# Hybrid encoder trunk: a fourth group of seven products in each FFN in place of blocks 4 and 5

## The chip, the cores and the metric

The kernel runs on one core of one Trainium2 chip. The metric is device microseconds (us) of one execution; three executions of the kernel before were timed, and a fourth was recorded by the profiler.

## The reference, cut to what matters

A trunk of two layers over 256 tokens of width 1024, all in float32. Each layer has a mixing part (two attention branches, merged) and a gated FFN with 2816 hidden columns. The change lies in the FFN alone:

```python
gate, up = jnp.split(rms_norm(h, g_ffn_pre) @ w_ffn_in, 2, axis=-1)
h = h + rms_norm((jax.nn.silu(gate) * up) @ w_ffn_out, g_ffn_post)
```

`w_ffn_in` is 1024 x 5632 (gate and up beside each other), `w_ffn_out` is 2816 x 1024. The hidden columns are cut into 11 blocks of 256, numbered 0 to 10.

## The kernel before, in words

**Three matmuls for one.** To keep float32 accuracy each operand is held as a high and a low part. The high part is a cast by ACT (`split`, line 113, in the trace `CAST wh_..`), the low part a subtraction by DVE (line 109, `TENSOR_TENSOR wl_..`). A product of two such operands is three matmuls: high by high, high by low, low by high (`mm3`). Every weight that comes from memory passes through ACT and then DVE in this way, in two halves of 1024 columns each.

**Units.** Weights come in units of 1 MB, 128 partitions by 2048 columns. A stream (`Stream`, named `ws`) loads them in the order of a list, `plan`. A plain load goes into one of two buffers (`raw_..`), so that a load waits until the unit two places ahead has been split. The split parts lie in four buffers each (`wh_..`, `wl_..`); a unit's buffers come free when PE has used it. `ws.depth` and `ws.held` keep at most four of them in use.

**The three kinds of work in the FFN.** The letters in the string `FFN` give their order; a `p` only loads a few small tensors.

- `u`: half of a plain block of `w_ffn_in` (one of two units), 24 matmuls of 128x512.
- `o`: one unit of `w_ffn_out` (`out_step`), 24 matmuls, 12 for each half of the tokens. It reads a block of the hidden activations, transposed, which `hid.need` fetches; which block is the next is set by `OUT`.
- `1` to `7`: a group of seven products (`seven`), which does two blocks (a pair, named by its first) in the manner of Strassen and Winograd: 7 products of 12 matmuls in place of 8. The activations' four combined forms are made once (`sums`). The weights' combinations are made in place, in `Stream.step`: with the four units of a pair called x, z (first half of the rows, gate and up), q and y (second half), the unit x is split for product 1, z is added to it by DVE (line 292), it is split again for product 2, y is added by DVE, it is split for product 3, then q is added to it from memory by an accumulating DMA of GpSimd (line 308, two halves), and it is split a last time for product 7. Product 4 uses y, product 6 uses q, product 5 uses z, to which y has been added by another accumulating DMA (line 295).

x and z have no buffers of their own: they are lent one of the four `wh` and one of the four `wl` buffers (in the trace `lent_..`). The `lend` flag lets the next pair's x and z be loaded only behind the split for product 7 of the pair before. y has a buffer of the kind `big_..`, and q one of the two `raw_..` buffers.

A pair's result is gated on ACT and DVE (lines 1339 and 106), turned by a DMA transpose (line 414) with copies by ACT before and behind it (lines 408 and 427), and split (`big_0ffnin`) for the `o` that reads it. `tick` and `need` decide where this is written in the program; the last pair (`PAIRS[-1]`) is turned by PE instead.

In each layer the blocks 0 and 1 come first, outside of the string. Before the change, 4, 5 and 10 are plain, and the groups start at 2, 6 and 8. What of `OUT` has not been used inside the string (three units) follows behind it, as `ffnout`.

**What sets the order.** Dependencies are found by the tile framework, and a scheduler writes each engine's instructions in one fixed order. On the chip each engine runs its own list in that order.

Of the kernel before, what the change touches and what calls it, by code (L numbers as in the profile page):

```python
# [34 lines left out]

FFN = "uu1u2u34u567" "uo12o34o5o67" "poo12o345o67"
MERGE = "GGGG1G2G34G5G67gggg"
PLAIN, PAIRS = (4, 5, 10), (2, 6, 8)  # L40
OUT = (0, 1, 2, 3, 4, 5, 10, 6, 7, 8, 9)

WAIT_LAST = (3, 4)
SENT, LANDED, NEXT = 3, 9, 2
# [7 lines left out]
def trunk_kernel(ctx: ExitStack, tc: tile.TileContext, a: dict, out: bass.AP):  # L52
# [87 lines left out]
    def unit(w, kh, c0):  # L140

        return lambda t: [
            (
                t[:, :2048].rearrange("p (k c) -> p k c", c=512),
                w[kh * 512 : (kh + 1) * 512, c0 : c0 + 512].rearrange("(k p) c -> p k c", p=P),
            )
        ]
# [24 lines left out]
            )  # L172
        ]

    plan = []
    for l in range(DEPTH):
        w = a["w_in"][l]
        plan += [unit_rows(w, n, C_RA, C_RA + 1056, 2 if l + n == 0 else 1) for n in range(4)]
        for c0 in (C_AK, C_GQ, C_GK, C_GV, C_GV + 512, C_GG, C_GG + 512):
            plan += [unit(w, kh, c0) for kh in range(2)]  # L180
        gates = [unit(w, kh, c0) for c0 in (C_GA, C_GA + 512, C_GB, C_GB + 512) for kh in range(2)]
        glas = [unit(a["w_o_gla"][l], kh, j * 512) for j in range(2) for kh in range(2)]
        pair = [unit(a["w_o_attn"][l], kh, j * 512) for kh in range(2) for j in range(2)]
        for x in MERGE:
            plan.append(gates.pop(0) if x == "G" else glas.pop(0) if x == "g" else (pair, int(x)))
        plan += [unit(a["w_out"][l], kh, j * 512) for kh in range(2) for j in range(2)]
        w = a["w_ffn_in"][l]
        blocks = [[unit_gate_up(w, kh, b) for kh in range(2)] for b in range(NBLK)]
        plan += blocks[0] + blocks[1]
        plains = [u for b in PLAIN for u in blocks[b]]  # L190
        pairs = [[unit(w, kh, c + b * 256) for kh in range(2) for c in (0, HIDDEN)] for b in PAIRS]
        outs = [unit_rows(a["w_ffn_out"][l], n) for n in OUT]
        for x in FFN.replace("p", ""):
            if x == "1":
                pair = pairs.pop(0)
            plan.append(plains.pop(0) if x == "u" else outs.pop(0) if x == "o" else (pair, int(x)))
        plan += outs
        plan += [unit_rows(a["w_ple_proj"][l], 0)]
        plan += [unit(a["w_ple_gate"][l], kh, j * 512) for kh in range(2) for j in range(2)]
# [14 lines left out]
    class Stream:  # L214
# [8 lines left out]
        def __init__(self, depth):  # L223
            self.depth, self.held, self.room, self.ready, self.open = depth, 0, 0, [], False
            self.loads, self.jobs, self.lend = [], [], False
            pairs = {}
            for item in plan:
                if callable(item):
                    x = Load(item)
                    self.loads.append(x)  # L230
                    self.jobs.append(lambda x=x: self.plain(x))
                else:
                    units, n = item
                    if n == 1:
                        b11, b12, b21, b22 = units
                        x, z = (Load(b, lambda tag=tag: self.lent(tag), tag == "wh") for b, tag in ((b11, "wh"), (b12, "wl")))
                        y, q = Load(b22, big), Load(b21)
                        pairs[id(units)] = x, y, z, q
                        self.loads += [x, y, z]
                    if n == 5:  # L240
                        self.loads.append(q)
                    self.jobs.append(lambda p=pairs[id(units)], n=n: self.step(n, *p))

        def lent(self, tag):

# [40 lines left out]
            for piece in self.put(x):  # L286
                self.cast = split(*piece)

        def step(self, n, x, y, z, q):
            def add(to, other):  # L290
                c = slice(0, 2048)
                nc.vector.tensor_tensor(out=to.raw[:, c], in0=to.raw[:, c], in1=other.raw[:, c], op=ALU.add)

            def sent(to, src):
                nc.gpsimd.dma_start(to.raw[:, :2048], src, accum_op=ALU.add)

            if n == 7:
                self.load()
            self.made((x, x, x, y, z, q, x)[n - 1])
            if n == 1:  # L300
                add(x, z)
                sent(z, y.raw[:, :2048])
            elif n == 2:
                add(x, y)
            elif n == 3:
                for dst, src in q.make(x.raw):
                    for c in (slice(0, 2), slice(2, 4)):
                        nc.gpsimd.dma_start(dst[:, c], src[:, c], accum_op=ALU.add)
            elif n == 7:
                self.held -= 1  # L310
                self.lend = True
# [499 lines left out]
    for l in range(DEPTH):  # L811
# [561 lines left out]
        steps, pairs, seven_ = chain.from_iterable(block(b) for b in PLAIN), list(PAIRS), None  # L1373
        for x in FFN:
            if x == "p":
# [6 lines left out]
            if x == "o":  # L1382
                n, w = outs.pop(0), ws.take()
# [118 lines left out]
```

## Time and profile before

| what | us |
|---|---|
| median of three executions (lowest, highest) | 918.69 (918.22, 921.97) |
| the profiled execution: its own time | 921.25 |
| the profiled execution: span from the first to the last instruction | 919.1 |
| PE busy in the span | 904.6 |
| DVE busy | 737.2 |
| ACT busy | 643.9 |
| GpSimd busy | 112.4 |

The page gives for each engine how long it was busy in the span. A busy PE is counted from the start of the first to the modelled end of the last of matmuls that overlap, so two neighbouring matmuls must be compared by their starts. Rows of the timeline have the start, the duration, the engine, the line, the operation, what is written and read, and, in brackets, how long the engine had been idle and what ended it. Layer 0's FFN runs from about 256 to 433 us, and its part with the groups from 280 to 415 us.

### The profile page before, as it was taken

Reading aid. Unit: us, or ns where it says so; the run is one execution under the profiler, and the core shown is the slowest. Engines: PE = TensorE matmul, PEld = TensorE weight load, DVE = VectorE, ACT = ScalarE, POOL = GpSimd, SP = SyncE. Lnnn points to the kernel's source line nnn. Section 1 sums busy time; section 2 is a strip of 40 time slices with the busy share of each in tenths; the row PEclk is TensorE's granted clock in tenths of the full one; section 3 lists DMA queues with packets and bytes.
Section 4 is the critical chain, followed back from the end, with each engine's and each line's share of the span. In section 5 each row is a group of like instructions: output and inputs, shape, how many; then the busy total and the mean of one; then the engine's idle time right before and its main releaser. Section 6 shows DMA issues by size and latency. Waiting matters only on the chain.

```text
span 919.1 us, 12313 instructions
## 1 busy us (share of the span) xinstructions
PE 904.6 (98%) x4561; PEld 768.3 (84%) x4561; DVE 737.2 (80%) x947; ACT 643.9 (70%) x1032; POOL 112.4 (12%) x174
## 2 busy tenths in 40 slices
PE   8999999999999999999999999999999999999996
PEld 6999888888888888888899988888888788878786
DVE  4798987977679796888689789688786798968874
ACT  4658777964568796776665686878656787957663
POOL 2410201140010100010023002111001010101000
PEclk9999999999999999999999999999999999999999
DMA  6555356986489998966555524399675999979541
GB/s 218 182 193 180 117 163 231 229 241 234 144 243 256 279 273 250 301 194 240 184 176 184 190 91 148 128 290 234 208 247 173 274 230 290 261 284 243 200 167 46
DMA packets 123290, 193.38 MB, mean 210 GB/s; under 512 B 33431, under 2 KB 56471, under 8 KB 122206
## 3 DMA queue, kind: packets, MB, share of 16 engines
q1 hardware_dynamic: 117726, 175.81, 59.3%
q0 software_dynamic: 5504, 16.78, 10.1%
q8 instruction: 36, 0.59, 0.3%
q14 instruction: 24, 0.20, 0.1%
HBM read 175.80 MB, written 1.05 MB: 192 GB/s over the span
## 4 chain that ended last, share of the span: by engine, by line
PE 80%; ACT 6%; DMA 5%; DVE 4%; issue 2%; POOL 2%; SPq 0%; POOLq 0%; ACTq 0%; DVEq 0%
PE acc_0ffnin L97 10%; PE acc_1ffnin L97 10%; PE acc_0ffnin L581 5%; PE acc_1gate L97 5%; PE acc_0gate L97 5%; PE acc_1ffnin L581 4%; PE acc_1gqk L97 3%; PE acc_0rq L97 2%; PE acc_0gqk L97 2%; PE acc_1ple L97 2%; PE acc_1gg L97 2%; PE acc_0gg L97 2%; PE acc_0v L97 2%; PE acc_1v L97 2%; PE acc_1merge L97 2%; PE acc_0merge L97 2%
## 5 line engine op out<-in xcount | busy, mean ns | idle before, releaser
L97 PE MATMUL acc_1ffnin<-wh_1ffnin,big_1ffnin 128*128 128x512 f32 x176 | 56.5, 392 | 0.1
L97 PE MATMUL acc_0ffnin<-wh_0ffnin,big_0ffnin 128*128 128x512 f32 x176 | 56.2, 391 | 0.0
L109 DVE TENSOR_TENSOR wl_1ffnin<-raw_1ffnin,wh_1ffnin 128x1024 fp32r<-128x1024 f32 x38 | 44.9, 1220 | 12.3 <-ACT wh_1ffnin L113 12.3
L109 DVE TENSOR_TENSOR wl_0ffnin<-raw_0ffnin,wh_0ffnin 128x1024 fp32r<-128x1024 f32 x38 | 44.9, 1221 | 10.5 <-ACT wh_0ffnin L113 10.2
L113 ACT CAST wh_1ffnin<-raw_1ffnin 128x1024 fp32r<-128x1024 f32 x38 | 38.3, 1050 | 17.7 <-DMA raw_1ffnin<-in_w_ffn_out_dram 9.1
L113 ACT CAST wh_0ffnin<-raw_0ffnin 128x1024 fp32r<-128x1024 f32 x38 | 38.4, 1050 | 16.8 <-DMA raw_0ffnin<-in_w_ffn_out_dram 7.8
L109 DVE TENSOR_TENSOR wl_1ffnin<-lent_1ffnin,wh_1ffnin 128x1024 fp32r<-128x1024 f32 x30 | 35.5, 1220 | 4.9 <-ACT wh_1ffnin L113 4.7
L109 DVE TENSOR_TENSOR wl_0ffnin<-lent_0ffnin,wh_0ffnin 128x1024 fp32r<-128x1024 f32 x30 | 35.5, 1221 | 4.8 <-ACT wh_0ffnin L113 4.7
L97 PEld LDWEIGHTS acc_1ffnin<-wh_1ffnin,big_1ffnin 128*128 128x128 f32 x176 | 33.0, 188 | 7.2 <-ACT wh_1ffnin L113 0.5
L97 PEld LDWEIGHTS acc_0ffnin<-wh_0ffnin,big_0ffnin 128*128 128x128 f32 x176 | 33.0, 188 | 6.9 <-DVE big_0ffnin L109 0.2
L113 ACT CAST wh_1ffnin<-lent_1ffnin 128x1024 fp32r<-128x1024 f32 x30 | 30.3, 1049 | 8.6 <-issue 2.9
L113 ACT CAST wh_0ffnin<-lent_0ffnin 128x1024 fp32r<-128x1024 f32 x30 | 30.3, 1050 | 8.4 <-issue 2.9
L97 PE MATMUL acc_1ffnin<-wl_1ffnin,big_1ffnin 128*128 128x512 f32 x88 | 34.4, 391 | 0.8 <-DVE wl_1ffnin L109 0.8
L97 PE MATMUL acc_0ffnin<-wl_0ffnin,big_0ffnin 128*128 128x512 f32 x88 | 34.5, 392 | 0.3 <-DVE wl_0ffnin L109 0.3
L581 PE MATMUL acc_0ffnin<-wh_0ffnin,mid_0ffnin 128*128 128x512 f32 x96 | 31.0, 390 | 0.0
L581 PE MATMUL acc_1ffnin<-wh_1ffnin,mid_1ffnin 128*128 128x512 f32 x96 | 31.0, 390 | 0.0
L97 PE MATMUL acc_0ffnin<-wh_0ffnin,big_0wout 128*128 128x512 f32 x96 | 30.4, 389 | 0.0
L97 PE MATMUL acc_1ffnin<-wh_1ffnin,big_1wout 128*128 128x512 f32 x96 | 30.3, 389 | 0.0
L97 PE MATMUL acc_0rq<-wh_start,big_start 128*128 128x384 f32 (+1 forms) x96 | 25.4, 350 | 1.5 <-ACT big_start L124 1.5
L97 PE MATMUL acc_1rq<-wh_0ple,big_0ple 128*128 128x384 f32 (+1 forms) x96 | 23.5, 325 | 0.0
L581 PE MATMUL acc_1ffnin<-wh_1ffnin,big_1wout 128*128 128x512 f32 x72 | 23.1, 389 | 0.0
L581 PE MATMUL acc_0ffnin<-wh_0ffnin,big_0wout 128*128 128x512 f32 x72 | 23.1, 389 | 0.0
(745 smaller groups left out, 3011.7 us busy)
## 6 DMA issues: line engine op xcount, KB each, us to landing
raw_0ffnin<-in_w_ffn_out_dram SPq DMA_DIRECT2D x11, 1024.0 KB, 5.1
raw_1ffnin<-in_w_ffn_out_dram SPq DMA_DIRECT2D x11, 1024.0 KB, 5.1
lent_0ffnin<-in_w_ffn_in_dram SPq DMA_DIRECT2D x6, 1024.0 KB, 7.5
lent_1ffnin<-in_w_ffn_in_dram SPq DMA_DIRECT2D x6, 1024.0 KB, 6.0
raw_0rq<-in_w_in_dram SPq DMA_DIRECT2D x4, 1024.0 KB, 5.1
raw_0v<-in_w_in_dram SPq DMA_DIRECT2D x4, 1024.0 KB, 5.1
raw_0merge<-in_w_out_dram SPq DMA_DIRECT2D x4, 1024.0 KB, 5.2
raw_0wout<-in_w_ffn_in_dram SPq DMA_DIRECT2D x8, 512.0 KB, 4.6
```

The lines of the kernel that those rows point to most:

```text
L97: return nc.tensor.matmul(o, lhsT, rhs, start=start, stop=stop)
L109: nc.vector.tensor_tensor(out=out, in0=in0, in1=in1, op=ALU.subtract)
L113: cast = nc.scalar.copy(hi, src)
L581: nc.tensor.matmul(o, x, y, start=first and k + n == 0, stop=k == 3 and n == 2, skip_group_check=not first)
```

## The change

Two constants of order are new, and a switch for how q is added:

```diff
-FFN = "uu1u2u34u567" "uo12o34o5o67" "poo12o345o67"
+FFN = "uu12o34o567" "o123o4567" "po123o4567" "o123o4567"
-PLAIN, PAIRS = (4, 5, 10), (2, 6, 8)
-OUT = (0, 1, 2, 3, 4, 5, 10, 6, 7, 8, 9)
+PLAIN, PAIRS = (10,), (2, 4, 6, 8)
+ADDED = (2, 4, 6, 8)
+OUT = (0, 1, 10, 2, 3, 4, 5, 6, 7, 8, 9)
...
-            elif n == 3:
+            elif n == 3 and far:
                 for dst, src in q.make(x.raw):
                     for c in (slice(0, 2), slice(2, 4)):
                         nc.gpsimd.dma_start(dst[:, c], src[:, c], accum_op=ALU.add)
+            elif n == 5 and not far:
+                add(x, q)
```

`far` is true for a pair that is in `ADDED`, and for the pair in the merge. All four pairs of the FFN are in `ADDED`, so every pair has its q added by the DMA, as before, and the last branch is never taken.

Blocks 4 and 5 become a fourth pair. In each layer 2 plain blocks (4 units, 96 matmuls) give way to 7 products (84 matmuls). The first group now has two `u` and two `o` between its products, the other three have one `o` ahead of product 1 and one between products 3 and 4. Three units of `w_ffn_out` are left for behind the string, as before.

The lists of the engines show the passage from one group to the next. The first place is DVE in layer 0, from the split for product 7 of the second group to the split for product 4 of the third. Before, `wl_0ffnin_3353` is product 7, `3359` and `3411` are two `o`, `3441`, `3482`, `3542` and `3566` are products 1 to 4, `3513` is an `o`, and lines 292 are the two additions:

```order
L109 TENSOR_TENSOR wl_0ffnin_3353<-lent_0ffnin_3023,wh_0ffnin_3352 128x1024 x2
L109 TENSOR_TENSOR wl_0ffnin_3359<-raw_0ffnin_3305,wh_0ffnin_3358 128x1024 x2
L625 TENSOR_TENSOR mid_0ffnin_3179<-acc_0ffnin_3396,mid_0ffnin_3179 128x512
L109 TENSOR_TENSOR wl_0ffnin_3411<-raw_0ffnin_3350,wh_0ffnin_3410 128x1024 x2
L106 TENSOR_TENSOR t_0ffnin_3418<-mid_0ffnin_3180,t_0ffnin_3418 128x512
L109 TENSOR_TENSOR wl_0ffnin_3441<-lent_0ffnin_3364,wh_0ffnin_3440 128x1024 x2
L106 TENSOR_TENSOR t_0ffnin_3435<-mid_0ffnin_3179,t_0ffnin_3435 128x512
L292 TENSOR_TENSOR lent_0ffnin_3364<-lent_0ffnin_3364,lent_0ffnin_3368 128x2048
L109 TENSOR_TENSOR wl_0ffnin_3482<-lent_0ffnin_3364,wh_0ffnin_3481 128x1024 x2
L292 TENSOR_TENSOR lent_0ffnin_3364<-lent_0ffnin_3364,big_0ffnin_3366 128x2048
L109 TENSOR_TENSOR wl_0ffnin_3513<-raw_0ffnin_3370,wh_0ffnin_3512 128x1024 x2
```

Now product 7 is `wl_0ffnin_3199`, `3205` the one `o` that follows, `3248`, `3278`, `3318` and `3364` are products 1 to 4, and `3343` is the `o` between 3 and 4 (the lines of the code have moved by one to six):

```order
L110 TENSOR_TENSOR wl_0ffnin_3199<-lent_0ffnin_2975,wh_0ffnin_3198 128x1024 x2
L110 TENSOR_TENSOR wl_0ffnin_3205<-raw_0ffnin_3108,wh_0ffnin_3204 128x1024 x2
L110 TENSOR_TENSOR mid_0ffnin_3085<-mid_0ffnin_3085,acc_0ffnin_3087 128x512
L631 TENSOR_TENSOR mid_0ffnin_3085<-acc_0ffnin_3233,mid_0ffnin_3085 128x512
L107 TENSOR_TENSOR t_0ffnin_3255<-mid_0ffnin_3086,t_0ffnin_3255 128x512
L110 TENSOR_TENSOR wl_0ffnin_3248<-lent_0ffnin_3210,wh_0ffnin_3247 128x1024 x2
L107 TENSOR_TENSOR t_0ffnin_3272<-mid_0ffnin_3085,t_0ffnin_3272 128x512
L296 TENSOR_TENSOR lent_0ffnin_3210<-lent_0ffnin_3210,lent_0ffnin_3214 128x2048
L110 TENSOR_TENSOR wl_0ffnin_3278<-lent_0ffnin_3210,wh_0ffnin_3277 128x1024 x2
L296 TENSOR_TENSOR lent_0ffnin_3210<-lent_0ffnin_3210,big_0ffnin_3212 128x2048
L110 TENSOR_TENSOR wl_0ffnin_3318<-lent_0ffnin_3210,wh_0ffnin_3317 128x1024 x2
L110 TENSOR_TENSOR wl_0ffnin_3343<-raw_0ffnin_3216,wh_0ffnin_3342 128x1024 x2
```

One `o` is gone from between products 7 and 1, and the `o` from between the second addition and product 3. The subtraction that takes product 5's sum out of `acc_0ffnin_3087`, into which PE then adds product 7, now stands behind the split of the `o`.

The second place is ACT at the same passage: the casts for products 2 and 3, and the copies of the sums that PE has finished. Before, `wh_0ffnin_3481` is the cast for product 2, `3512` for an `o`, `3541` for product 3; L629 and L632 copy out products 1 and 2:

```order
L113 CAST wh_0ffnin_3481<-lent_0ffnin_3364 128x1024 x2
L113 CAST wh_0ffnin_3512<-raw_0ffnin_3370 128x1024 x2
L427 COPY mid_0ffnin_3459<-mid_0ffnin_3459 128x2x512
L629 COPY mid_0ffnin_3520<-acc_0ffnin_3522 128x512
L113 CAST big_0ffnin_3537<-mid_0ffnin_3459 128x4x128
L113 CAST wh_0ffnin_3541<-lent_0ffnin_3364 128x1024 x2
L427 COPY mid_0ffnin_3473<-mid_0ffnin_3473 128x2x512
L632 COPY mid_0ffnin_3520<-acc_0ffnin_3523 128x512
```

Now L635 and L638 are these copies, `wh_0ffnin_3277` and `3317` the casts for products 2 and 3, `3342` that for the `o`, `3363` and `3386` those for products 4 and 5, and `big_0ffnin_3382` the second group's result, which this `o` reads:

```order
L635 COPY mid_0ffnin_3325<-acc_0ffnin_3327 128x512
L114 CAST wh_0ffnin_3277<-lent_0ffnin_3210 128x1024 x2
L638 COPY mid_0ffnin_3325<-acc_0ffnin_3328 128x512
L114 CAST wh_0ffnin_3317<-lent_0ffnin_3210 128x1024 x2
L114 CAST wh_0ffnin_3342<-raw_0ffnin_3216 128x1024 x2
L114 CAST wh_0ffnin_3363<-big_0ffnin_3212 128x1024 x2
L433 COPY mid_0ffnin_3295<-mid_0ffnin_3295 128x2x512
L640 COPY mid_0ffnin_3326<-acc_0ffnin_3327 128x512
L114 CAST big_0ffnin_3382<-mid_0ffnin_3295 128x4x128
L114 CAST wh_0ffnin_3386<-lent_0ffnin_3214 128x1024 x2
```

The copies of products 1 and 2 now stand ahead of the casts for products 2 and 3, where before each stood behind the cast of the product that follows it.

The third place is PE, a little further on. Before, PE ran the `o` of the string whole. Now the `o` behind product 3 (`wh_0ffnin_3342`) starts when half of product 4 (`wh_0ffnin_3363`) is done:

```order
L587 MATMUL acc_0ffnin_3328<-wl_0ffnin_3364,mid_0ffnin_2712 128x512
L587 MATMUL acc_0ffnin_3328<-wh_0ffnin_3363,mid_0ffnin_2712 128x512
L98 MATMUL acc_0ffnin_2860<-wh_0ffnin_3342,big_0ffnin_3382 128x512
L98 MATMUL acc_0ffnin_2860<-wl_0ffnin_3343,big_0ffnin_3382 128x512
L98 MATMUL acc_0ffnin_2861<-wh_0ffnin_3342,big_0ffnin_3382 128x512
```

Its first 12 matmuls run there, and its other 12, for the second half of the tokens, behind most of the rest of product 4. In the second to fourth groups PE also runs 12 matmuls of the `o` that follows a group between products 6 and 7. Layer 1 has the same lists but for a place or two.

More of the change, by code (lines that the diff above doesn't have):

```diff
@@ L173, in unit_rows @@
         ]
-    plan = []
+    plan, added = [], []
     for l in range(DEPTH):
@@ L183, in trunk_kernel @@
         pair = [unit(a["w_o_attn"][l], kh, j * 512) for kh in range(2) for j in range(2)]
+        added.append(id(pair))
         for x in MERGE:
@@ L195, in trunk_kernel @@
                 pair = pairs.pop(0)
+                if PAIRS[-1 - len(pairs)] in ADDED:
+                    added.append(id(pair))
             plan.append(plains.pop(0) if x == "u" else outs.pop(0) if x == "o" else (pair, int(x)))
@@ L241, in __init__ @@
                         self.loads.append(q)
-                    self.jobs.append(lambda p=pairs[id(units)], n=n: self.step(n, *p))
+                    self.jobs.append(lambda p=pairs[id(units)], n=n, f=id(units) in added: self.step(n, f, *p))
         def lent(self, tag):
@@ L287, in made, with step @@
                 self.cast = split(*piece)
-        def step(self, n, x, y, z, q):
+        def step(self, n, far, x, y, z, q):
             def add(to, other):
```

## The prediction

> **What bounds the kernel now.** I read the page's first lines, then who PE waits for, then the stretch with the groups by windows, and last the timelines of PE, DVE and ACT around one passage between two groups.
>
> ```profile
> span 919.1 us, 12313 instructions
> PE 904.6 (98%) x4561; PEld 768.3 (84%) x4561; DVE 737.2 (80%) x947; ACT 643.9 (70%) x1032; POOL 112.4 (12%) x174
> ```
>
> PE is busy 98% of the span: PE sets the time. In the windows with the groups (279 to 415 us in layer 0, 740 to 866 in layer 1) PE's waits are these alone:
>
> ```profile
> PE acc_0ffnin L97 <- DVE wl_0ffnin L109: 0.3, 1, 0.3
> PE acc_1ffnin L97 <- DVE wl_1ffnin L109: 0.8, 1, 0.8
> ```
>
> So 0.3 and 0.8 us: splits arrive in time. But not by much, as the windows of layer 0's three groups show (columns: length, then busy time of PE, PEld, DVE, ACT, POOL, granted clock, DMA share, GB/s):
>
> ```profile
> 279.00:326.00 47.00, 47.00 (x209) 38.91 (x209) 41.19 (x45) 38.10 (x53) 3.42 (x3) 1.00 0.97 255
> 326.00:373.00 47.00, 46.73 (x207) 38.38 (x206) 38.18 (x38) 34.68 (x42) 3.29 (x3) 1.00 0.92 282
> 373.00:415.00 42.00, 42.00 (x189) 34.78 (x188) 37.22 (x34) 31.44 (x36) 4.31 (x4) 1.00 0.85 235
> ```
>
> DVE works 37 to 41 of 42 to 47 us, ACT 31 to 38, and the DMA share is 0.85 to 0.97. PE is the bound, with three others close behind. What decides is the passage between groups. PE in the third group, first matmuls of product 6 of the group before, then of products 1, 2 and of the `o` behind them:
>
> ```profile
> 367.78 0.39 PE L581 MATMUL acc_0ffnin<-wh_0ffnin,big_0wout 128*128 128x512 f32 x1
> ...
> 384.10 0.39 PE L581 MATMUL acc_0ffnin<-wh_0ffnin,big_0wout 128*128 128x512 f32 x1
> ...
> 386.82 0.39 PE L581 MATMUL acc_0ffnin<-wh_0ffnin,mid_0ffnin 128*128 128x512 f32 x1
> ...
> 389.54 0.39 PE L97 MATMUL acc_0ffnin<-wh_0ffnin,big_0ffnin 128*128 128x512 f32 x1
> ```
>
> From 384.10 to 386.82 there are 12 matmuls: 2.72 us for a product, 0.227 for a matmul, 5.44 for a unit of 24. Product 7 began at 367.78 + 2.72 = 370.50. DVE for the same passage: the split for product 7, for product 1, a gating, the first addition, the split for product 2, the second addition, a split of transposed results, and the split for product 3:
>
> ```profile
> 366.30 2.35 DVE L109 TENSOR_TENSOR wl_0ffnin<-lent_0ffnin,wh_0ffnin 128x1024 fp32r<-128x1024 f32 x2
> ...
> 375.82 2.36 DVE L109 TENSOR_TENSOR wl_0ffnin<-lent_0ffnin,wh_0ffnin 128x1024 fp32r<-128x1024 f32 x2
> 378.09 0.69 DVE L106 TENSOR_TENSOR t_0ffnin<-mid_0ffnin,t_0ffnin 128x512 f32<-128x512 f32 x1
> 378.70 2.29 DVE L292 TENSOR_TENSOR lent_0ffnin<-lent_0ffnin,lent_0ffnin 128x2048 f32<-128x2048 f32 x1
> 382.18 2.36 DVE L109 TENSOR_TENSOR wl_0ffnin<-lent_0ffnin,wh_0ffnin 128x1024 fp32r<-128x1024 f32 x2 [1.19 <-ACT wh_0ffnin L113]
> 384.58 2.29 DVE L292 TENSOR_TENSOR lent_0ffnin<-lent_0ffnin,big_0ffnin 128x2048 f32<-128x2048 f32 x1
> ...
> 389.06 0.69 DVE L109 TENSOR_TENSOR big_0ffnin<-mid_0ffnin,big_0ffnin 128x512 fp32r<-128x512 f32 x1
> 389.66 2.36 DVE L109 TENSOR_TENSOR wl_0ffnin<-lent_0ffnin,wh_0ffnin 128x1024 fp32r<-128x1024 f32 x2
> ```
>
> A split takes 378.09 - 375.82 = 2.27 us, its first half, which is enough for a product to begin, about 1.2. Product 2's split starts 6.4 us after product 1's: addition, then ACT's cast, then DVE again, with 1.19 of DVE idle. This chain is longer than the 2.72 us of a product. It is hidden because PE has two units between products 7 and 1 (10.9 us) and one between 2 and 3 (5.44). Splits 1, 2 and 3 end 6.0, 2.4 and 3.4 us before PE's start of their product; the last start is 389.54 + 5.44 and a short transpose, some 395.3.
>
> **The change, part by part.** *Removed and added matmuls.* Per layer 96 go and 84 come: 12 x 0.227 = 2.7 us less on PE, 5.4 for both layers. This is on the path, as PE waits for nothing now.
>
> *Work on DVE and ACT.* A group with two `o` has nine splits: 9 x 2.27 + 2 x 2.29 + some seven operations of 512 columns at 378.70 - 378.09 = 0.61: 29.3 us, against 132 matmuls x 0.227 = 30.0 on PE. DVE would be busy 98% with no freedom left. That alone costs nothing, but every late piece stays late.
>
> *DMA.* Window 326 to 373, and where the next x and z are issued:
>
> ```profile
> q1 hardware_dynamic: 7116, 11.13, 67.1%
> q0 software_dynamic: 688, 2.10, 24.4%
> ...
> 367.97 0.92 SPq L263 DMA_DIRECT2D lent_0ffnin<-in_w_ffn_in_dram  x2
> ...
> lent_0ffnin<-in_w_ffn_in_dram POOLq DMA_DIRECT2D x6, 512.0 KB, 9.8
> ```
>
> Plain loads cost 0.671 x 47 / 11.13 = 2.83 us per MB (transposes counted in), the accumulating ones of a group 0.244 x 47 = 11.5 us. The new group moves six plain units of 1.05 MB: 17.8 + 11.5 = 29.3 us in 30.0. This too just fits. In SP's queue x and z stay behind an `o`'s load as now, and product 7's accumulation needs some 12 us from product 3's split (9.8 to land, and two issues), where PE has the `o`, products 4, 5 and 6: 5.44 + 3 x 2.72 = 13.6. I cost it at nothing, since the stalls below lengthen this cover; without it, 0 to 2 us a group.
>
> *The passage.* x can be loaded only when the split for product 7 is over (here 366.30 + 2.27 = 368.6; the issue is at 368.0), and product 1's split ended 9.5 us after that. The chain from there does not change. What changes is what PE has meanwhile: one unit instead of two before product 1, none between 2 and 3. ACT's rows for products 1 and 2, for an old result, the copy of product 1, a cast of old results, and the cast for product 3:
>
> ```profile
> 374.53 2.00 ACT L113 CAST wh_0ffnin<-lent_0ffnin 128x1024 fp32r<-128x1024 f32 x2
> ...
> 381.10 2.00 ACT L113 CAST wh_0ffnin<-lent_0ffnin 128x1024 fp32r<-128x1024 f32 x2 [1.23 <-DVE lent_0ffnin L292]
> ...
> 386.26 1.35 ACT L427 COPY mid_0ffnin<-mid_0ffnin 128x1024 uint16<-128x1024 uint16 x1
> 387.47 0.58 ACT L629 COPY mid_0ffnin<-acc_0ffnin 128x512 f32<-128x512 f32 x1
> 387.94 0.63 ACT L113 CAST big_0ffnin<-mid_0ffnin 128x512 fp32r<-128x512 f32 x1
> 388.46 2.01 ACT L113 CAST wh_0ffnin<-lent_0ffnin 128x1024 fp32r<-128x1024 f32 x2
> ```
>
> With these I lay the same passage for the new lists:
>
> - Product 1: wanted at 370.50 + 2.72 + 5.44 = 378.7, its first half is ready at 375.82 + 1.2 = 377.0. No wait.
> - Product 2: wanted at 381.4, ready at 382.18 + 1.2 = 383.4: 2.0 late. In the third and fourth groups the copy of product 1 stands ahead of the cast: 381.4, some 0.2 of PE's pipeline, 0.5 copy, 1.0 first cast, 1.2 first half on DVE, 0.1 of signals: 384.4, 3.0 late. Mean 2.6.
> - Product 3: behind the start of product 2, the other half of its split 1.15, addition 2.2, cast 1.2, half a split 1.2: 5.8 us, against 2.72: 3.0 late. By ACT's list (copy of product 2 ahead of the cast) 2.9.
> - Product 4 and the `o`: DVE still has half a split (1.1), the split of the `o` (2.27) and half of product 4's: 4.6 after product 3's start, 1.9 late. The `o`'s two halves wait for the old group's results, each behind one more split on DVE and a copy and a cast of 1.2 and 0.5 on ACT: 0.8 together. Sum 2.7; between 0 (nothing waited there before) and 4.5.
> - The end of the group: product 6's split stands behind a subtraction that needs product 4's sum, then come product 7's split and half of the next `o`'s: 1.1 late, 2.2 where its buffer is the one that product 7 leaves. And product 7 waits for a subtraction behind that split. I take 1.4; between 0 and 2.8.
>
> Together 2.6 + 3.0 + 2.7 + 1.4 = 9.7 us for a passage. The first group keeps a `u` or `o` between 2 and 3 and its x is loaded early: nothing there. Three passages a layer, two layers: 6 x 9.7 = 58.2, less 5.4: 52.8 us slower. Nothing gives this back, as PE has no other work to take forward in its list. The span goes from 919.1 to 971.9; the profiled execution's own time was 921.25, 2.2 more than its span and 2.6 above the median. On the median 918.69 the sum gives 971.5; I say 971.
>
> *Bounds.* Below: only products 2 and 3, at 2.0 and 2.9: 6 x 4.9 - 5.4 = 24, 943. Above: 3.4, 3.2, 4.5 and 2.8: 6 x 13.9 - 5.4 = 78, 997.
>
> **Rivals.** *Faster: the splits keep ahead.* If the split for product 7 came 6 us before PE's product 7 instead of 370.50 - 368.6 = 1.9, the chain would be hidden, and 5.4 us stay: 913.3. For it speaks the quiet list of waits; against it, that four split buffers, one of them lent, let product 7 be split only when PE has done product 4, and that DVE has no time over. The Trainium skill ("Perfetto Trace Analysis", section "Identifying the Most-Contended Engine") says to optimize the engine with the highest occupancy first, TensorE judged by its weight loads; those are 84% here, DVE 80%, and by this rule the change would be the 5.4 us gain. The rows above bear that out for the average only. Chance 0.05.
>
> *Only the DMA binds.* The chain is shorter than I lay it, and the group takes 31 to 33 us instead of 30.0: 6 x 1 to 6 x 3 less 5.4: 919 to 931. Chance 0.06.
>
> *The clock falls.* At the start of the trace, and somewhat later, the steps between matmuls of 384 columns are these:
>
> ```profile
> 11.56 0.53 PE L97 MATMUL acc_0rq<-wh_start,big_start 128*128 128x384 f32 x1
> 11.88 0.53 PE L97 MATMUL acc_0rq<-wl_start,big_start 128*128 128x384 f32 x1
> ...
> 18.73 0.34 PE L97 MATMUL acc_0rq<-wl_start,big_start 128*128 128x384 f32 x1
> 18.91 0.51 PE L97 MATMUL acc_0rq<-wh_start,big_start 128*128 128x384 f32 x2
> ```
>
> 0.32 against 0.18 us: PE ran at about half speed for some 7 us. If each passage brought that back, half of 7 us is lost in each: 6 x 3.5 = 21 more, 992. The Trainium skill ("TensorE: Matmul & The Clock Gate", section "HAM oscillation") has the clock halved after idle gaps over some 3.4 us. My gaps are at most 3.0 each, so by that rule it just does not happen, but the clock's windows above never saw such gaps. Chance 0.12.
>
> **How the numbers follow.** My sum within its bounds has 0.72, faster 0.05, DMA alone 0.06, the clock 0.12, and 0.05 is left for more than all this (late accumulations on top). The prediction is 971. The range 946 to 996 leaves out the first two rivals and the ends of the bounds, and takes in the clock. About 0.5% is what a measurement here can tell from no change: faster 0.05, same 0.02 (from the DMA case), slower 0.93.
>
> **What would show it.** Starts of products 1, 2 and 3 in groups two to four 5 to 6 us apart instead of 2.72; PE's waits led by the low parts of the products, some 5 to 6 us a group, and then by the `o` behind product 4; each layer's groups about 26 us longer (29.1 less 2.7) than the 136 us of the windows above; a DMA share near 0.8; a granted clock of 1.00. It is wrong if the starts are 2.7 apart, or if the first group stalls as the others do.

## The result: 967.8 us, 5.3% slower, and the profile after

The changed kernel takes 967.77 us (median of four, 967.09 to 970.8), the kernel before 919.61 beside it. The ratio is 1.0527, with a 95% interval from 1.0494 to 1.056. The profiled execution has a span of 965.6 us, 46.5 more than before.

The page's first lines of the changed kernel, and its row of the granted clock in 40 slices:

```profile
span 965.6 us, 12315 instructions
...
PE 924.9 (96%) x4537; PEld 771.2 (80%) x4537; DVE 764.6 (79%) x965; ACT 658.1 (68%) x1042; POOL 121.1 (13%) x180
...
PEclk9999999999999999989999999999999999987999
```

PE has 24 matmuls less and yet is busy 20 us longer, in part because there are slices in which its clock was not full. The waits of PE in the groups, which before were 0.3 and 0.8 us (engine and line, what it waited for: us in total, times, longest):

```profile
PE acc_1ffnin L587 <- ACT wh_1ffnin L114: 9.2, 5, 2.0
PE acc_0ffnin L587 <- ACT wh_0ffnin L114: 9.0, 5, 2.0
PE acc_0ffnin L587 <- DVE wl_0ffnin L110: 5.4, 8, 1.5
PE acc_1ffnin L587 <- DVE wl_1ffnin L110: 3.9, 7, 0.8
```

L587 is the line of the products. All of these waits lie in groups two to four, at products 2, 3 and 4; as a rule the first matmul waits for a cast, the second for its subtraction. The windows with the groups (columns as in the prediction):

```profile
279.00:445.00 166.00, 150.57 (x615) 116.52 (x614) 132.64 (x127) 114.58 (x137) 14.34 (x13) 0.95 0.82 230
751.00:916.00 165.00, 151.16 (x606) 117.75 (x604) 131.03 (x125) 112.51 (x136) 13.41 (x12) 0.93 0.84 229
```

No engine is busy all the time, the DMA share is 0.82 and 0.84 where it had been 0.85 to 0.97, and the granted clock is 0.95 and 0.93. From the first unit's start to the end of product 7 of the last group, less what stood there of the units behind the string, it is 134.3 us before and 159.4 now in layer 0, 135.2 and 160.0 in layer 1: 25 us a layer.

The starts of product 1 in groups two to four of layer 0 (timeline of PE) show the new beat:

```profile
324.56 0.39 PE L587 MATMUL acc_0ffnin<-wh_0ffnin,big_0wout 128*128 128x512 f32 x1
...
362.02 0.39 PE L587 MATMUL acc_0ffnin<-wh_0ffnin,big_0wout 128*128 128x512 f32 x1
...
401.14 0.39 PE L587 MATMUL acc_0ffnin<-wh_0ffnin,big_0wout 128*128 128x512 f32 x1
```

A group takes 37.5 and 39.1 us, in which PE has 132 matmuls, 30.0 us. What makes it 38 is seen on DVE: the split for product 3 of the second group, and then the splits for product 7, and for products 1, 2 and 3 of the third; between them, at 348.20, a subtraction that needs product 4's sum:

```profile
333.65 2.36 DVE L110 TENSOR_TENSOR wl_0ffnin<-lent_0ffnin,wh_0ffnin 128x1024 fp32r<-128x1024 f32 x2 [1.16 <-ACT wh_0ffnin L114]
...
348.20 0.69 DVE L110 TENSOR_TENSOR mid_0ffnin<-acc_0ffnin,mid_0ffnin 128x512 f32<-128x512 f32 x1 [3.09 <-PE acc_0ffnin L587]
...
351.08 2.35 DVE L110 TENSOR_TENSOR wl_0ffnin<-lent_0ffnin,wh_0ffnin 128x1024 fp32r<-128x1024 f32 x2
...
360.36 2.36 DVE L110 TENSOR_TENSOR wl_0ffnin<-lent_0ffnin,wh_0ffnin 128x1024 fp32r<-128x1024 f32 x2 [2.07 <-ACT wh_0ffnin L114]
...
366.69 2.36 DVE L110 TENSOR_TENSOR wl_0ffnin<-lent_0ffnin,wh_0ffnin 128x1024 fp32r<-128x1024 f32 x2 [1.17 <-ACT wh_0ffnin L114]
...
372.55 2.36 DVE L110 TENSOR_TENSOR wl_0ffnin<-lent_0ffnin,wh_0ffnin 128x1024 fp32r<-128x1024 f32 x2 [1.17 <-ACT wh_0ffnin L114]
```

On ACT, the cast for product 6, then a copy of the finished group's gated result and the cast for product 1; on SP, the loads of the next x and z:

```profile
347.52 2.00 ACT L114 CAST wh_0ffnin<-raw_0ffnin 128x1024 fp32r<-128x1024 f32 x2 [3.14 <-PE acc_0ffnin L98]
...
358.33 1.05 ACT L414 COPY t_0ffnin<-t_0ffnin 128x1024 uint16<-128x1024 uint16 x1 [0.76 <-DVE t_0ffnin L107]
359.28 2.00 ACT L114 CAST wh_0ffnin<-lent_0ffnin 128x1024 fp32r<-128x1024 f32 x2
...
353.46 0.92 SPq L267 DMA_DIRECT2D lent_0ffnin<-in_w_ffn_in_dram  x2
```

From product 3 to product 3 it is 17.4 + 9.3 + 6.3 + 5.9 = 38.9 us, and it is one closed round trip. Split 3 lets PE do products 3 and 4 and the `o`; the end of the `o` (L98, the 3.14 us) frees the buffer for the cast of product 6, and the end of product 4 releases the subtraction ahead of split 6; then come splits 6 and 7; behind split 7 the next x is loaded, while DVE and ACT gate the first half of the finished group's result; then split 1, addition, split 2, addition, split 3.

Some of these links run beside each other and end close together. What ends last ahead of split 1 is here not the load: the cast for product 1 (359.28) starts when ACT is through with the copy, which had waited for DVE. It is so in three of the four passages out of groups two and three; in the fourth ACT waits another 0.2 us for the load. In run 5 below the x at this place had landed at 355.31, and its cast began at 356.45, behind the same copy.

Before, product 1 of the third group began 46.8 us after that of the second (384.10, and the start below), since PE had that much to do:

```profile
337.30 0.39 PE L581 MATMUL acc_0ffnin<-wh_0ffnin,big_0wout 128*128 128x512 f32 x1
```

That a trip of this length went round unseen there is borne out by run 2.

### The profile page after: what moved, and what is told of

The parts are those of the page before. It is cut to its first block, busy times and chain, and to the rows that moved or that the text cites. A ratio compares the mean times of both kernels' runs of the same rounds, so it can differ in the third digit from the quotient of the medians.

```text
span 965.6 us, 12315 instructions
## 1 busy us (share of the span) xinstructions
PE 924.9 (96%) x4537; PEld 771.2 (80%) x4537; DVE 764.6 (79%) x965; ACT 658.1 (68%) x1042; POOL 121.1 (13%) x180
## 4 chain that ended last, share of the span: by engine, by line
PE 66%; DVE 11%; ACT 10%; DMA 7%; issue 4%; POOL 2%; SPq 0%; ACTq 0%; POOLq 0%; DVEq 0%
PE acc_1ffnin L98 7%; PE acc_1ffnin L587 5%; PE acc_0gate L98 5%; PE acc_1gate L98 5%; DVE wl_0ffnin L110 4%; PE acc_0ffnin L98 3%; ACT wh_0ffnin L114 3%; PE acc_1gqk L98 2%; PE acc_0gqk L98 2%; PE acc_0rq L98 2%; PE acc_1ple L98 2%; PE acc_0gg L98 2%; PE acc_1gg L98 2%; PE acc_1v L98 2%; PE acc_0v L98 2%
## 5 line engine op out<-in xcount | busy, mean ns | idle before, releaser
L110 DVE TENSOR_TENSOR wl_1ffnin<-lent_1ffnin,wh_1ffnin 128x1024 fp32r<-128x1024 f32 x40 | 47.3, 1221 | 18.6 <-ACT wh_1ffnin L114 18.6
L110 DVE TENSOR_TENSOR wl_0ffnin<-lent_0ffnin,wh_0ffnin 128x1024 fp32r<-128x1024 f32 x40 | 47.3, 1222 | 18.3 <-ACT wh_0ffnin L114 18.3
L587 PE MATMUL acc_1ffnin<-wh_1ffnin,mid_1ffnin 128*128 128x512 f32 x128 | 49.0, 450 | 9.2 <-ACT wh_1ffnin L114 9.2
L98 PE MATMUL acc_0ffnin<-wh_0ffnin,big_0ffnin 128*128 128x512 f32 x176 | 57.5, 395 | 0.1
L98 PE MATMUL acc_1ffnin<-wh_1ffnin,big_1ffnin 128*128 128x512 f32 x176 | 56.9, 393 | 0.1
L587 PE MATMUL acc_0ffnin<-wh_0ffnin,mid_0ffnin 128*128 128x512 f32 x128 | 46.8, 432 | 9.0 <-ACT wh_0ffnin L114 9.0
L587 PEld LDWEIGHTS acc_1ffnin<-wh_1ffnin,mid_1ffnin 128*128 128x128 f32 x128 | 28.6, 223 | 17.8 <-ACT wh_1ffnin L114 11.7
L587 PEld LDWEIGHTS acc_0ffnin<-wh_0ffnin,mid_0ffnin 128*128 128x128 f32 x128 | 27.0, 211 | 17.2 <-ACT wh_0ffnin L114 11.6
L98 PEld LDWEIGHTS acc_0ffnin<-wh_0ffnin,big_0ffnin 128*128 128x128 f32 x176 | 33.0, 188 | 9.4 <-ACT big_0ffnin L114 1.6
L98 PEld LDWEIGHTS acc_1ffnin<-wh_1ffnin,big_1ffnin 128*128 128x128 f32 x176 | 33.0, 188 | 8.6 <-ACT big_1ffnin L114 1.3
L98 PE MATMUL acc_0ffnin<-wl_0ffnin,big_0ffnin 128*128 128x512 f32 x88 | 34.9, 397 | 0.8 <-DVE wl_0ffnin L110 0.6
L98 PE MATMUL acc_1ffnin<-wl_1ffnin,big_1ffnin 128*128 128x512 f32 x88 | 34.6, 395 | 0.6 <-DVE wl_1ffnin L110 0.4
L587 PE MATMUL acc_0ffnin<-wl_0ffnin,mid_0ffnin 128*128 128x512 f32 x64 | 28.7, 449 | 5.5 <-DVE wl_0ffnin L110 5.4
L587 PE MATMUL acc_1ffnin<-wl_1ffnin,mid_1ffnin 128*128 128x512 f32 x64 | 29.9, 466 | 3.9 <-DVE wl_1ffnin L110 3.9
L587 PE MATMUL acc_1ffnin<-wh_1ffnin,big_1wout 128*128 128x512 f32 x96 | 31.4, 389 | 0.0
L587 PE MATMUL acc_0ffnin<-wh_0ffnin,big_0wout 128*128 128x512 f32 x96 | 31.4, 389 | 0.0
```

The costliest lines, as they stand in the source:

```text
L98: return nc.tensor.matmul(o, lhsT, rhs, start=start, stop=stop)
L110: nc.vector.tensor_tensor(out=out, in0=in0, in1=in1, op=ALU.subtract)
L587: nc.tensor.matmul(o, x, y, start=first and k + n == 0, stop=k == 3 and n == 2, skip_group_check=not first)
```

## The experiments

Theory A is the prediction's: the spacing of the string uncovers waits of a fixed size at products 2 and 3. B: a fourth group costs this wherever the units stand. C: the half clock is a loss of its own. D, in run 4: DVE's work as a whole sets the end of a group. E, the round trip, was formed from runs 1 to 7. In the diffs `...` stands for code left out.

### 1. The units respaced, four groups

```diff
-FFN = "uu12o34o567" "o123o4567" "po123o4567" "o123o4567"
+FFN = "12u34567" "uo12o34567" "oo12o34567" "poo12o34567"
```

> Four groups as in the changed kernel, but the units in between stand as the three groups had them: two units ahead of product 1 and one between products 2 and 3 in groups two to four (one between 2 and 3 in the first). Theory A (the prediction's: the chain from the split for product 7 to the split for product 3 is uncovered by the spacing): the waits of 2.6 and 3.0 us at products 2 and 3 go, the 24 matmuls saved stay: 919 - 5.4 = 913 to 925. Theory B (a fourth group costs this much wherever the units stand, by its two more accumulating transfers and additions, the DMA above all): 935 to 965. Theory C (the half clock alone is the loss): no gaps, no half clock, the same 913 to 925, so A and C aren't told apart here.

954.37 us, ratio 1.0379 (1.0348 to 1.041). A is missed by 30 us, and B's range holds. More than half of the miss is this string's own: the first group lost its two units ahead, and from the wait ahead of its product 1 to the second group's product 1 it takes 47.0 us for 156 matmuls (35.4 us), 11.6 us too much in each layer. But in the next two groups of layer 0 the waits at products 2 and 3 are gone, and from product 1 to product 1 it is still 38.4 and 39.4 us, now with 35.4 us of PE work in it:

```profile
326.06 0.39 PE L587 MATMUL acc_0ffnin<-wh_0ffnin,big_0wout 128*128 128x512 f32 x1
...
364.47 0.39 PE L587 MATMUL acc_0ffnin<-wh_0ffnin,big_0wout 128*128 128x512 f32 x1
...
403.83 0.39 PE L587 MATMUL acc_0ffnin<-wh_0ffnin,big_0wout 128*128 128x512 f32 x1
```

The waits sit at the `o` behind products 2 and 6 instead. In layer 1 the two groups take 41.7 and 37.8 us.

### 2. Three groups, but close

```diff
-FFN = "uu1u2u34u567" "uo12o34o5o67" "poo12o345o67"
+FFN = "uu1u2u34u567" "uooooo123o4567" "po123o4567"
```

(in the kernel before, nothing else)

> The kernel before with its three groups and six plain units, only the units respaced: the second and third group in the close form (1, 2, 3 in a row, one unit between 3 and 4, one between 7 and the next 1, five units ahead of the second group). No group is added and no matmul less. Theory A: the spacing alone costs per close group what the prediction laid for a passage, bounds 4.9 to 9.7, and 7.5 to 9 by the changed kernel's trace: four such passages, 919 + 4 x 8 = 951 (939 to 958). Theory B (the fourth group's own work): 915 to 925.

944.38 us, 1.0265 (1.0234 to 1.0296), 24.6 us slower with the same matmuls, within A's 939 to 958. No fourth group is needed for the loss, so it isn't B's in that form. The two groups are not alike: in the third, from product 1 to the `o` behind half of product 4, it is 18.6 us where 42 matmuls and four small transposes make 10.2; in the second, with five units ahead, products 2 and 3 wait only 1.0 us together (and the units ahead 2.9, for a block whose result they read too early). A close "123" alone costs little when enough work stands ahead of it. From the second group's split for product 3 to the third's, with 132 matmuls on PE, it is 37.2 us, the trip of the changed kernel:

```profile
366.49 2.36 DVE L109 TENSOR_TENSOR wl_0ffnin<-lent_0ffnin,wh_0ffnin 128x1024 fp32r<-128x1024 f32 x2 [1.12 <-ACT wh_0ffnin L113]
...
403.64 2.36 DVE L109 TENSOR_TENSOR wl_0ffnin<-lent_0ffnin,wh_0ffnin 128x1024 fp32r<-128x1024 f32 x2 [2.57 <-ACT wh_0ffnin L113]
```

### 3. Idle matmuls in the waits

```diff
+FILL = {2: (0, 0, 0), 4: (2, 9, 0), 6: (6, 8, 3), 8: (6, 8, 0)}
...
+                with tc.issue_after(last_mm[0].ins):
+                    mm(c[0], sp.tok(0, 0)[0], made[0][0].rearrange("p k t -> p (k t)"), True, True)
```

> The changed kernel with idle matmuls (of 512 columns, into a bank that product 6 starts anew) put on PE ahead of products 2 and 3 of groups two to four (2 and 9, 6 and 8, 6 and 8, and 3 ahead of product 4 in the third group: 0.45 to 2.0 us each, less than the wait there). They do no part of the result and only keep PE busy in its waits. Theory A (the chain on DVE and ACT sets when a passage ends; a slow PE is hidden in it): granted clock 1.00, time 962 to 970, as the waits that the slow matmuls had filled come back. Theory C (the half clock is a loss of its own): some 75 matmuls at half speed give back 0.227 us each, 17 us: 949 to 954.

964.86 us, 1.0493 (1.0465 to 1.0522). The window of layer 0's groups:

```profile
279.00:441.00 162.00, 151.98 (x649) 118.51 (x648) 130.32 (x124) 112.59 (x134) 14.35 (x13) 1.00 0.84 230
```

The clock stays at 1.00 and 2.9 us come back, less than the two intervals can part, and not C's 17. In the changed kernel the clock had been halved for 41 us in all. Three of these stretches:

```profile
406.40:420.00 13.60, 10.89 (x24) 7.73 (x25) 10.32 (x9) 7.76 (x9) 3.41 (x3) 0.50 0.60 108
...
846.70:853.50 6.80, 6.15 (x15) 4.82 (x16) 6.27 (x6) 6.38 (x9) 2.43 (x2) 0.50 0.61 86
880.80:894.50 13.70, 10.93 (x24) 7.80 (x25) 10.41 (x9) 7.84 (x9) 2.46 (x2) 0.50 0.59 106
```

All lie at these waits. Groups two and three take 37.6 and 39.5 us with the clock kept (37.5 and 39.1 without); only the last group is shorter, by 2.3 us by the starts. There the slow matmuls do hold up the trip: product 3 starts 7.9 us behind product 2 in the changed kernel (405.76 and 413.70) and 5.9 with the clock kept (406.27 and 412.12), since ACT copies the sum of product 2 ahead of the cast for product 3.

### 4. The additions in two halves

```diff
-                c = slice(0, 2048)
-                nc.vector.tensor_tensor(...)
+                for c in (slice(0, 1024), slice(1024, 2048)) if id(x) in halved else (slice(0, 2048),):
+                    nc.vector.tensor_tensor(...)
```

> The changed kernel with each addition of z and y to x in the FFN made in two halves of 1024 columns, so that ACT may cast the first half while DVE adds the second: the chain from split 1 to split 2 and from split 2 to split 3 is up to 1.1 us shorter each, the work the same (a little overhead on DVE). Theory A: six passages x 2 x 0.9 to 1.1 = 11 to 13 us less: 955. Theory C: the waits fall below what lowers the clock in most passages, and up to 17 us more come back: 938 to 950. Theory D (DVE's work as a whole sets the end of a group, not this chain): no change, 965 to 970.

947.18 us, 1.0308 (1.0279 to 1.0336), 20.6 us faster than the change. Groups two and three take 35.0 and 36.0 us, 2.5 and 3.2 less, and the clock is 0.999:

```profile
324.91 0.39 PE L590 MATMUL acc_0ffnin<-wh_0ffnin,big_0wout 128*128 128x512 f32 x1
...
359.92 0.39 PE L590 MATMUL acc_0ffnin<-wh_0ffnin,big_0wout 128*128 128x512 f32 x1
...
395.88 0.39 PE L590 MATMUL acc_0ffnin<-wh_0ffnin,big_0wout 128*128 128x512 f32 x1
```

The time lies in C's range, not at A's 955. But against run 3, which has the clock kept too, it is 17.7 us, 2.9 a passage, so the clock isn't what was gained; it is the chain, by somewhat more than A's two times 1.1. D falls: DVE's work is the same and the time is not.

### 5, 6, 7. The `o` between products 2 and 3; then halves; then q by DVE

```diff
-FFN = "uu12o34o567" "o123o4567" "po123o4567" "o123o4567"
+FFN = "uu12o34567" "o12o34567" "o12o34567" "po12o34567"
```

> The changed kernel with four groups, where the `o` that stood between products 3 and 4 stands between products 2 and 3 (and of the two in the first group one is left, so that four units follow behind the string instead of three; each `o` reads a block that is at least one group old). Theory A (chain from split 7 to split 3, uncovered by the spacing): product 3 is covered by 5.4 us, product 4 and the rest follow in 2.7 us steps as before the change, product 2 stays 2.6 late: a passage of 3 to 4 us instead of 9, 967 - 6 x 5.5 = 934 (928 to 940). Theory B (the group's transfers and additions as a whole, wherever the units stand): 950 to 967.

961.6 us, 1.0454 (1.0425 to 1.0482). This is what brought A down: product 3 waits for nothing any more, and the time hardly moves. Product 1 in groups two to four:

```profile
322.15 0.49 PE L587 MATMUL acc_0ffnin<-wh_0ffnin,big_0wout 128*128 128x512 f32 x1 [0.49 <-ACT wh_0ffnin L114]
...
359.20 0.39 PE L587 MATMUL acc_0ffnin<-wh_0ffnin,big_0wout 128*128 128x512 f32 x1
...
398.39 0.39 PE L587 MATMUL acc_0ffnin<-wh_0ffnin,big_0wout 128*128 128x512 f32 x1
```

37.1 and 39.2 us, the changed kernel's 37.5 and 39.1. The waits have moved to product 2 (4.3 us beyond its matmuls) and, in the third group, the `o` behind product 6 (4.8).

With the additions in halves as well:

> The same order, and each addition of the FFN in two halves. Theory A: product 2 is late by 1 to 1.5 us instead of 2.6, so 6 x 1.3 = 8 less: 926 (919 to 932); with nothing left to wait for it would end at 919 - 5 = 914. Theory B: 945 to 965. A third bound, the DMA: the four groups' transfers took 0.82 of the 166 us of the changed kernel, 136 us, against 134.5 us that the string took before the change, so not below 918.

954.8 us, 1.0378 (1.0361 to 1.0396): again not A's 926. And with `ADDED = ()`:

> The order and the halves of the run before, and q added to x by DVE behind the split for product 5 (the branch that the change brought and never took) instead of by the accumulating transfer from memory: 1 MB less for the DMA and 2.3 us more for DVE in each group. If the DMA binds what is left: 5 to 15 us below the run before. If DVE's time or its order binds: 4 x 2 x 1 to 2 us = 8 to 18 above it.

952.06 us, 1.0354 (1.0331 to 1.0377), 2.7 less than the run before, which the intervals don't tell apart, and neither of the two sizes expected. The groups take 35.6 and 35.1 us. DVE is busy 32.8 and 31.4 of them and stands still for some 2 us ahead of the split for product 1: with q on DVE the trip seems to run through DVE's list.

B's ranges hold in runs 1, 5 and 6; what speaks against it is run 2, and run 10 below for the transfers. E takes in both sides: where the units stand moves the waits, and the beat of some 37 to 39 us stays.

### 8, 9. The same idle work in two places

24 idle matmuls, 5.4 us, in groups two to four: ahead of product 1 (`FILL = (24, 0)`), or behind the `o`, ahead of the end of product 4 (`FILL = (0, 24)`).

```diff
+        filler(fill[0])
         times(a, quad(0, 0), True, lambda: nc.scalar.copy(p1, a))
...
         times(a, form(1), False, lambda: nc.scalar.copy(u, a))
         yield
+        filler(fill[1])
```

> The changed kernel with 24 idle matmuls (5.4 us of PE at full clock, no part of the result) directly ahead of product 1 in groups two to four. Theory E (formed from the runs before: each group is a round trip, split for product 3, PE's products 3, 4 and the `o`, a buffer free, splits 6 and 7, load of the next x, splits 1 to 3 with their additions, of 37 to 39 us against 30 us of PE work; the place just ahead of product 1 does not lie on it): the 33 us of added work on PE vanish in the waits at products 2 and 3, 964 to 976. Theory A (waits of a fixed size at products 2 and 3 from the spacing alone): product 2 is covered, product 3 in part, 5.4 - 2.6 - 2.5 a passage, 967 to 972, so A and E aren't told apart by this run alone. If PE's work itself set the time: 1000.

959.58 us, 1.0435 (1.0418 to 1.0453): with 33 us more work on PE the kernel is 8 us *faster* than the change, and faster than both E and A had it.

```profile
329.18 0.39 PE L591 MATMUL acc_0ffnin<-wh_0ffnin,big_0wout 128*128 128x512 f32 x1
...
366.63 0.39 PE L591 MATMUL acc_0ffnin<-wh_0ffnin,big_0wout 128*128 128x512 f32 x1
...
404.77 0.39 PE L591 MATMUL acc_0ffnin<-wh_0ffnin,big_0wout 128*128 128x512 f32 x1
```

The groups take 37.5 and 38.1 us, and PE's work fills 35.4 of each. The clock is at 0.999; that, by run 3, explains about 3 of the 8 us. The rest was not taken apart: the scheduler also put the `o` whole behind product 7 in two groups, and three quarters of product 4 instead of half ahead of the `o`.

> The same 24 idle matmuls, now behind the `o` and ahead of the end of product 4 in the same groups. Theory E: this place lies on the round trip (the subtraction for product 4 stands on DVE ahead of the splits for products 6 and 7), so nearly all of it is added: 967 + 6 x 4 to 5.4 = 991 to 1000. If any work of PE is hidden in a group that has 7 to 9 us of waits: 967 to 975.

990.89 us, 1.0778 (1.0756 to 1.08), 23 us slower than the change:

```profile
324.90 0.39 PE L591 MATMUL acc_0ffnin<-wh_0ffnin,big_0wout 128*128 128x512 f32 x1
...
367.28 0.39 PE L591 MATMUL acc_0ffnin<-wh_0ffnin,big_0wout 128*128 128x512 f32 x1
...
410.64 0.39 PE L591 MATMUL acc_0ffnin<-wh_0ffnin,big_0wout 128*128 128x512 f32 x1
```

42.4 and 43.4 us: here 4.9 and 4.2 of the 5.4 us were added to each, and some 1.2 to the last, behind which no further group has to come round. In all it is 23 of the 33 us, at the low edge of E's range. The scheduler put the `o` whole behind product 7 here too, in groups two and three. The same matmuls cost 23 us at one place of PE's list and nothing at the other, 31 us apart.

Fixed waits at products 2 and 3 alone would give much the same pair of times, as they too would be covered by work ahead of product 1 and not by work behind them. Taken with runs 1 and 5, where those waits went or moved and the beat stayed, the pair shows the round trip: what lies on it counts, what lies beside it is free.

### 10, 11. Without the transfer that adds q

Both leave out the accumulating transfer of q in the FFN's groups: the changed kernel (10), and the order of run 5 (11).

> The changed kernel without the accumulating transfer of q into x in the FFN groups (product 7 then lacks that term). The prediction cost this transfer at nothing, since it has landed (346.5 us in the third group's passage) before the split for product 7 comes to its turn (349.4). Theory E and the prediction: 960 to 968. If the transfer or the DMA's load held the group: 6 x 2 to 4 us less, 943 to 955.

968.22 us, 1.053 (1.0514 to 1.0546): no change. The transfer is off the trip, as the prediction had costed it, and with one 1 MB transfer less in each group the DMA isn't what sets the beat.

> The order with the `o` between products 2 and 3 (961.6 us), without that transfer. There the second half of the split for product 7 waits 0.6 us for it (landed 348.3, 12 us behind the split for product 3), and the `o`s load later. Theory E: the round trip of that order passes through this transfer instead of PE, and is 1 to 4 us shorter without it: 938 to 955. If the transfer is hidden there too: 958 to 964.

956.66 us, 1.0405 (1.0382 to 1.0429), 4.9 us less than run 5, at the edge of what the intervals tell apart, and between the two expectations. The groups take 36.3 and 35.3 us, 0.8 and 3.9 less. In that order the transfer lies on the trip in some of the groups.

### 12. The clock by itself

A kernel of its own that computes none of the result and copies x to the output: runs of matmuls, each waiting for an addition on DVE. It was run once.

> A kernel of its own that computes none of the result (it copies x to the output): runs of 24, 12 or 8 matmuls of 512 columns, each run waiting for a DVE addition of 500 to 2500 columns into its operand, ten times for each pair, with 48 matmuls ahead of each. Idle gaps from about 0.9 to 3.1 us. By the changed kernel's trace (half clock behind each stretch of 3.4 us with more than some 1.75 us idle, none behind 1.5 us): half clock in the stages with gaps above 1.8 us, full clock below, with all three lengths of run. By the rule of idle gaps over 3.4 us: full clock in all stages.

Windows of single stages (length, busy PE, PEld, DVE, POOL, granted clock, DMA share, GB/s). The DVE column tells the gap: nine additions of 13.62 us in all leave PE idle 1.6 us each time, nine of 17.36 us 2.0 (by the list of waits, 14.4 and 18.2 us in nine).

```profile
187.40:253.60 66.20, 51.75 (x218) 39.84 (x216) 13.62 (x9) 0.00 (x0) 1.00 0.00 1
271.80:349.60 77.80, 59.61 (x217) 45.63 (x216) 17.36 (x9) 0.00 (x0) 0.89 0.00 0
...
687.40:729.10 41.70, 27.25 (x110) 19.57 (x108) 13.62 (x9) 0.00 (x0) 1.00 0.00 0
744.60:802.00 57.40, 39.21 (x109) 27.98 (x108) 17.36 (x9) 0.00 (x0) 0.77 0.00 0
1065.00:1098.40 33.40, 18.94 (x73) 12.81 (x72) 13.63 (x9) 0.00 (x0) 1.00 0.00 0
1113.00:1159.30 46.30, 28.10 (x73) 18.52 (x73) 17.37 (x9) 0.00 (x0) 0.69 0.00 0
```

With runs of 24, 12 and 8 matmuls alike, gaps of 1.6 us leave the clock full and gaps of 2.0 us halve it part of the time. So it is in all eighteen stages: full in the nine with gaps up to 1.6 us, halved for part of the time in the nine with longer ones. The gaps of 2.0 us are far from 3.4 us.

## Why the prediction was right, and where it was not

**The total.** 971 was said, 967.8 measured. For a passage 9.7 us was said; by the starts of PE the six passages hold 7.5, 9.2 and 11.6 us (layer 0) and 7.5, 9.8 and 11.8 (layer 1) beyond their matmuls, 9.6 in the mean. The 24 matmuls saved are there, and the first group waits for almost nothing: 204 matmuls from 277.75 to 324.56, 46.8 us for 46.3.

Six times 9.6 less 5.4 would be 52.0, against 52.8 in the sum; the medians are only 48.2 apart, the spans 46.5. The strings grew by 49.9 us, since before the change they held about 1 and 2 us beyond their matmuls, which the prediction took as nothing. Another 2.4 us of the spans are none of the change: by the trace it begins layer 0's FFN at 253.80 instead of 256.21, ahead of everything that was changed.

**The terms.** They assumed a full clock, so they are measured in run 3, layer 0, with the idle matmuls counted as waiting:

| late, us | said | groups 2, 3, 4 | mean |
|---|---|---|---|
| product 2 | 2.6 (2.0, 3.0, 3.0) | 1.6, 3.5, 3.4 | 2.8 |
| product 3 | 3.0 | 3.4, 3.1, 3.1 | 3.2 |
| product 4 and the `o` | 2.7 | 2.3, 2.2, 2.3 | 2.3 |
| end of the group | 1.4 | 0.4, 0.7, 0.4 | 0.5 |
| sum | 9.7 | 7.6, 9.5, 9.2 | 8.8 |

The chain over ACT and DVE that was laid for products 2 and 3 held within 0.2 us in the mean, and within 0.5 in each group. Two terms were mis-sized. Product 4 and the `o` were 2.3 us late instead of 2.7, almost all of it at product 4: the `o` behind it is idle for 0.1 us at most. The end of the group was 0.5 instead of 1.4: product 6 waits for nothing, and the `o` behind it for 0.1 to 0.4 us. The halved clock, which the sum had left out, made up for most of this. That the mean comes within 0.1 us of the 9.7 is luck.

One reading of the prediction was off without harm: that x is loaded only when the split for product 7 is over. Its issue in the kernel before (367.97) comes 0.6 us ahead of that split's end (368.6), and by the trace it waited for an `o` on PE.

**"A granted clock of 1.00"** is the step that failed. The gaps were as said (at most 2.0 us idle, 2.8 with the second wait of the same product). The rule of the Trainium skill ("TensorE: Matmul & The Clock Gate", section "HAM oscillation") is no idle gaps of PE over about 3.4 us, and by it the clock would have stayed full. The measurement decides: run 12 has it halved at 2.0. The rival that had the clock fall had the amount right, six times 7 us, 42 against the 41 measured, but not the price, 21 us: keeping the clock up gave 2.9, since most of the slow matmuls only fill a wait that the trip imposes anyway. The last group is the exception, as run 3 shows.

**What PE waits for.** The low parts were to lead, with 5 to 6 us a group. The casts lead (18.2 us of the 27.5 in the list, the low parts 9.3), since the wait of a product's first matmul is for its first half cast; all told it is 4.6 us a group beside the slowed matmuls. The starts of products 1, 2 and 3 were to be 5 to 6 us apart. From product 2 to 3 they are 6.4, 5.9 and 7.9 in layer 0; from 1 to 2 only 2.7, 4.7 and 4.6, and in the second group the first matmul of product 2 doesn't wait at all, only its second. The DMA share near 0.8 came as said, and so did the groups: 25 us a layer, 26 said.

**Right sum, short reason.** The prediction read the waits as gaps of the string, "what changes is what PE has meanwhile". Runs 1, 5 and 6 put a unit back between 2 and 3, and the wait went elsewhere. The lateness in the sum is the difference between two numbers: the round trip, 37 to 39 us, which the prediction never added up, and PE's work for a group, 30.0, which it had. The beat is nearly the same in layer 0 with 30.0 us of PE work (the changed kernel, run 5) and with 35.4 (runs 1 and 8), in three different orders of the units. The change took PE's work per group from 46.8 us to below the trip, and the matmuls it saved, and more, came back as waiting. The three units more that stood in a group before, 16 us, had been the cover.

**What stays open.** Which part of the trip would have to go for four groups to pay was not settled. The fastest kernel with four groups here is run 4, 947.2, still 3.1% behind the kernel before, and none beats that. Loading the next x into a buffer of its own, ahead of split 7, wasn't tried. By the rows above it would gain little alone, since ACT's cast for product 1 stands behind the gating of the finished group; that the gating sets this link was not tested by a run either.

## What to carry to other kernels

Where a buffer is filled, changed in place and given back once a round, add up the round trip over all engines and queues and set it against the bounding engine's work per round: as long as the trip is the shorter it doesn't show, and work taken off the bounding engine is a gain only down to it. Waits read off one order say how much is late, not what would mend it; moving the waits by another order, and putting the same idle work on the trip and beside it, tells a trip from waits of a fixed size. In the profile such a trip looks like this: the bounding engine waits at the same places each round, and no other engine or queue is busy throughout.

## What the runs showed of the hardware

- The clock halved with no idle gap over 2.0 us. In run 12 nothing happened up to 1.6 us idle, and every stage with longer gaps had it (with gaps of 2.0 us 0.89, 0.77 and 0.69 instead of 1.00, for 5.4, 2.7 and 1.8 us of matmuls between the gaps). In the trace's records of the clock the halved stretches are 3.41 us long or multiples of it. That agrees with a window of that length which is judged on how much of it was busy, as the Trainium skill describes it ("TensorE: Matmul & The Clock Gate", section "What's actually happening"). By run 12 the border lies between 1.6 and 2.0 us idle in 3.41, about half of the window. The changed kernel's trace agrees: cut into stretches of 3.41 us in step with its clock records, the five ahead of a halving hold 1.9 to 2.6 us without a matmul, their several gaps added, and from 20 to 960 us no other stretch at full clock holds more than 1.62. The border at half is an estimate from these figures.
- Half clock for 41 us cost about 3 us in the changed kernel (run 3, less than the two intervals can part), since it fell into waits.
- Work that is no part of the result made a kernel faster: 33 us of idle matmuls ahead of product 1, with what the scheduler moved for them, 959.6 against 967.8 us.
